# Block 1's branch projections and embedding gate: from three 256-column matmuls on a shared bank to 512+256 columns on a bank per feature tile

## The chip, the cores and the metric

The kernel runs on one core of a Trainium2 chip. The metric is the device time of one execution in microseconds (us), as the median of several runs; lower is better. The engines are TensorE (PE for its matmuls, PEld for its weight loads), VectorE (DVE), ScalarE (ACT), GpSimd (POOL) and SyncE (SP, which issues the DMAs here).

## The reference, cut to what matters

A sequence of 256 tokens with 1024 features goes through two different transformer blocks in float32 (the second has two layers). The change lies in the first block, behind its attention:

```python
y_a = o_a @ w_branch_diff[i]          # o_a: [256, 512], out of the differential attention
y_b = o_b @ w_branch_moba[i]          # o_b: [256, 512], out of the block attention
merged = sigmoid(g_a) * y_a + sigmoid(g_b) * y_b
x = x + merged @ w_out[i]
x = x + sigmoid(x @ w_ple_gate[i]) * (p[i] @ w_ple[i])
```

After it the second block begins with `h = rmsnorm(x, g_mix[0])` and its wide input projection.

## The kernel before

Activations lie transposed: features on the 128 partitions, in 8 tiles of 128 features, the 256 tokens along the row. Every float32 product is made of three: each operand is split into a rounded high part (`F32R`) and the low rest, and hi*hi + hi*lo + lo*hi is summed in PSUM. A `Pair` tile holds high and low part of an activation tile side by side, 512 columns in all.

The weights come as a stream of 189 chunks of 1 MB (`chunks`). For every chunk the loop at the end of `tile_blocks` issues, in this order: the split of the chunk two further on (`split`: per half chunk a copy to `wh` on ACT, L286, and a subtraction to `wl` on DVE, L287), the fetch of the chunk five further on (an SP DMA), then the chunk's matmuls and what empties their banks, then one step of each open attention head (`threads`). A planner that simulates the engines writes the final order of each engine's queue, so work of neighbouring chunks and heads is interleaved on PE, and that order is fixed when the kernel runs.

PSUM has five banks for the chunks (`acc`, `NACC`) and three for the heads (`aux`). A chunk's matmuls take one of these forms:

- `mm_2` (L308, used by `chunk_2`, `branch1` and `ple`): two feature tiles share one bank, 256 columns each. For each k tile and each of the two, `mm3` (L131 to L133) issues three matmuls of 256 columns, each with its own weight load: `wh` on the high part, `wh` again on the low part, `wl` on the high part. The bank then holds finished sums.
- `mm_t` (L292, used by `chunk_t`): a feature tile has a bank of its own. `wh` is loaded once and multiplies high and low part in one matmul of 512 columns (L300), `wl` multiplies the high part in one of 256 columns (L303). The sum for a token is then the sum of the bank's two halves, which `fold` makes: a copy of one half to SBUF on ACT (L320), and an addition of the other on DVE (L321). With `fresh` the two kinds alternate k tile by k tile, otherwise all 512-column ones come first.
- `mm_n` (L343): tokens on the partitions, for values and for keys and queries of block 1, always 512 columns.

Block 1 behind its attention: four chunks `branch1(c)`, each with two feature tiles of both branch projections (four k tiles each); the chunk `ple` (`p @ w_ple`); four chunks of `w_out`, whose emptying adds to the residual `X` and writes the new `X` as a `Pair` (tag A2) with `hilo` (L127, L128); four chunks of `w_ple_gate`; then block 2's first projections, which read the `Pair` X2 that `norm_tile` (L196, L197, and the squares at L205, L207) writes. Before the change, `branch1` multiplies the sigmoids `ga`, `gb` with the banks on DVE (L626, L627), adds them on POOL (L628) and splits the result (L127, L128), 512 columns at a time. `pleg_evac` takes the sigmoid of the bank on ACT (`act`, L114), multiplies it with the embedding term `pw` (L706) and adds it to `X` (L707), 512 columns at a time, and then calls `norm_tile` for both feature tiles. In block 2 the same merge is done in the other form, by `ret_evac` and `sb_evac` with `merge_tile` (L609, L610).

Of the kernel before, what the change touches and what calls it, by code (L numbers as in the profile page):

```python
# [12 lines left out]
AF = mybir.ActivationFunctionType  # L13
# [8 lines left out]
S = 256  # L22
D = 1024
KT = 8
# [52 lines left out]
def tile_blocks(ctx: ExitStack, tc: tile.TileContext, a: dict, out: bass.AP):  # L77
    nc = tc.nc
    V, A, G, T = nc.vector, nc.scalar, nc.gpsimd, nc.tensor
# [6 lines left out]
    def tl(shape, tag, dt=F32, bufs=1):  # L86
        uid[0] += 1
        return pool.tile([P] + list(shape), dt, tag=tag, bufs=bufs, name=f"{tag}_{uid[0]}")
# [12 lines left out]
    def acc():  # L101
        uid[0] += 1
        return psp.tile([P, 512], F32, tag="acc", bufs=NACC, name=f"acc_{uid[0]}")
# [3 lines left out]
    def act(o, i, func, **kw):  # L107

        need = "sigmoid" if func == AF.Sigmoid else "natural_log_exp"
        if table[0] != need:  # L110
            table[0] = need
            ld = A.preload_act_table_set(need + "_and_others")
            tc.stamp_issue_order_token(ld.ins, "act_table")
        ins = A.activation(o, i, func, **kw)  # L114
        tc.stamp_issue_order_token(ins.ins, "act_table")

    def f32(ap):
        return ap.bitcast(F32)
# [7 lines left out]
    def hilo(hi, lo, src):  # L126
        A.activation(hi, src, AF.Copy)  # L127
        V.tensor_sub(lo, src, f32(hi))  # L128

    def mm3(o, lh, ll, rh, rl, start, stop):  # L130
        T.matmul(o, lhsT=lh, rhs=rh, start=start, stop=False, skip_group_check=True)  # L131
        T.matmul(o, lhsT=lh, rhs=rl, start=False, stop=False, skip_group_check=True)  # L132
        T.matmul(o, lhsT=ll, rhs=rh, start=False, stop=stop, skip_group_check=True)  # L133
# [52 lines left out]
    def new_norm(g, sub=None):  # L186
        n = Norm()
        n.g, n.sub = g, sub
        n.x = Pair("X2")
        n.sq = tl([S], "sq")  # L190
        n.sq2 = tl([S], "M2") if sub is not None else None
        return n

    def norm_hilo(n, x, k):

        A.activation(n.x.h[:, k], x, AF.Copy, scale=n.g[:, k:k + 1])  # L196
        V.scalar_tensor_tensor(n.x.l[:, k], x, n.g[:, k:k + 1], f32(n.x.h[:, k]), ALU.mult, ALU.subtract)  # L197

    def norm_square(n, X, k):

        for sq, kw in ((n.sq, {}), (n.sq2, {"scale": n.sub[:, k:k + 1]} if n.sub is not None else {})):
            if sq is None:
                continue
            t = sq if k == 0 else tl([S], "f", bufs=NF)
            A.activation(t, X[:, k], AF.Square, **kw)  # L205
            if k:
                (V if k == KT - 1 else G).tensor_add(sq, sq, t)  # L207

    def norm_tile(n, X, k):
        norm_hilo(n, X[:, k], k)  # L210
        norm_square(n, X, k)
# [43 lines left out]
    chunks = []  # L255
# [10 lines left out]
    def wcols(w, c, k0=0, kt=KT, n=S):  # L266
        return w, k0 * P, kt, c * n
# [21 lines left out]
    def mm_t(ch, ks, xs, j0, evac, n=2):  # L289

        for j in range(n):
            ps, w = acc(), slice((j0 + j) * P, (j0 + j + 1) * P)
            kinds = [[(i, n) for i in range(len(ks)) for n in range(2)]] if ch.fresh else \
                [[(i, n) for i in range(len(ks))] for n in range(2)]
            for i, n_ in sum(kinds, []):
                k, x = ks[i], xs[i]
                if n_ == 0:
                    T.matmul(ps, lhsT=ch.wh[:, k, w], rhs=x.rearrange("p c t -> p (c t)"), start=i == 0, stop=False,  # L300
                             skip_group_check=True)
                else:
                    T.matmul(ps[:, 0:S], lhsT=ch.wl[:, k, w], rhs=x[:, 0], start=False, stop=i == len(ks) - 1,  # L303
                             skip_group_check=True)
            run_pre()
            evac(ps, j)

    def mm_2(ch, ks, xs, j0=0, n=2):  # L308

        ps = acc().rearrange("p (j t) -> p j t", j=2)  # L310
        for i, (k, x) in enumerate(zip(ks, xs)):
            for j in range(2):
                w = slice((j0 + j) * P, (j0 + j + 1) * P)
                mm3(ps[:, j], ch.wh[:, k, w], ch.wl[:, k, w], x[:, 0], x[:, 1], i == 0 and j == 0, i == len(ks) - 1)
        return ps

    def fold(ps, out=None):

        t = tl([S], "f", bufs=NF) if out is None else out
        A.activation(t, ps[:, S:2 * S], AF.Copy)  # L320
        V.tensor_add(t, t, ps[:, 0:S])  # L321
        return t
# [25 lines left out]
    def run_pre():  # L348
        while pre:
            with tc.high_priority():  # L350
                pre.pop(0)()

    def chunk_t(w, c, x, evac, k0=0, fresh=False):
        def go(ch):
            mm_t(ch, range(KT), [x().t[:, k] for k in range(KT)], 0, lambda ps, j: evac(ps, 2 * c + j))
        chunks.append(Chunk([wcols(w, c, k0)], go))
        chunks[-1].fresh = fresh

    def chunk_2(w, c, x, evac, k0=0):
        def go(ch):  # L360
            ps = mm_2(ch, range(KT), [x().t[:, k] for k in range(KT)])
            run_pre()
            evac(ps, c)
        chunks.append(Chunk([wcols(w, c, k0)], go))

    def chunk_n(w, c, x, evac, k0=0, parts=1):
        ps = []

        def go(ch):
            if not ps:  # L370
                ps.extend([acc() for _ in range(parts)] for _ in range(2))
                if ch is chunks[0]:
                    mm_k(ch, ps, x(), 0)
                    return
                for h in range(2):
                    mm_n(ch, ps[h], x(), 0, h)
                return
            for h in range(2):
                mm_n(ch, ps[h], x(), 4, h)
                run_pre()  # L380
                evac(ps[h] if parts > 1 else ps[h][0], h)
        for half in range(2):
            chunks.append(Chunk([wcols(w, c, k0 + 4 * half, 4, 512)], go, (4, 512)))


    class Values:
# [5 lines left out]
        def evac(self, ps, h):  # L392
            r = st.n.rc[h]
            A.activation(self.h[:, h], ps, AF.Copy, scale=r)
            V.scalar_tensor_tensor(self.l[:, h], ps, r, f32(self.h[:, h]), ALU.mult, ALU.subtract)
# [3 lines left out]
    X = tl([KT, S], "X")  # L399
    n0 = new_norm(g_norm)  # L400
    st.n = n0
    x_ = lambda: st.n.x
# [197 lines left out]
    def sig(store, c, i):  # L600
        s = store[(c, i)]
        if not s[1]:
            act(s[0], s[0], AF.Sigmoid)
            s[1] = True
        return s[0]

    def merge_tile(k, pb, ga, gb):
        t = fold(pb)
        V.tensor_mul(t, t, gb)  # L609
        V.tensor_add(t, t, ga)  # L610
        hilo(mg.x.h[:, k], mg.x.l[:, k], t)

    gates1 = {}
    mg = Norm()

    def start_merge():
        mg.x = Pair("M2")

    def branch1(c):
        def go(ch):  # L620
            if c == 0:
                start_merge()
            xs = [a1.t[:, k] for k in range(8)]
            ga, gb = sig(gates1, c, 0), sig(gates1, c, 1)
            pa, pb = mm_2(ch, range(4), xs[0:4]), mm_2(ch, range(4, 8), xs[4:8])
            V.tensor_mul(ga, ga, pa)  # L626
            V.tensor_mul(gb, gb, pb)  # L627
            G.tensor_add(ga, ga, gb)  # L628
            k = slice(2 * c, 2 * c + 2)
            hilo(mg.x.h[:, k], mg.x.l[:, k], ga)  # L630
            if c == 1:
                threads.append(ple_in())
        chunks.append(Chunk([wcols(("w_branch_diff", 0), c, 0, 4), wcols(("w_branch_moba", 0), c, 0, 4)], go))
# [12 lines left out]
    def ple_in():  # L646

        pn = scr[:, 0:512].rearrange("p (j t) -> p j t", j=2)
        load(pn, a["pt"])
        yield  # L650
        pt_.x = Pair("vh", 2)
        hilo(pt_.x.h, pt_.x.l, pn)
        yield
# [43 lines left out]
            if k % 2:  # L697
                yield

    def pleg_evac(ps, c):  # L700
        if c == 0:
            nxt.n = new_norm(gfm, g_fin)
        k = slice(2 * c, 2 * c + 2)
        t = tl([2, S], "sig", bufs=4)
        act(t, ps, AF.Sigmoid)
        V.tensor_mul(t, t, pw[:, k])  # L706
        V.tensor_add(X[:, k], X[:, k], t)  # L707
        for j in range(2):
            norm_tile(nxt.n, X, 2 * c + j)
        if c == 3:  # L710
            st.n = nxt.n
            pre.append(rotary_scales)
            threads.append(first_out())

    nxt = Norm()
    for c in range(4):
        chunk_2(("w_ple_gate", 0), c, x_, pleg_evac)


    def ret_head(h, j, qk, v, L):  # L720
# [374 lines left out]
```

## Time and profile before

| what | value |
|---|---|
| median of 3 runs | 1169.01 us (1168.88 to 1169.1) |
| profiled execution, its own time | 1168.73 us |
| its span, from the first instruction to the last | 1167.0 us |
| mean granted TensorE clock in it | 0.997 |
| PE busy | 1155.9 us, 99% of the span |
| DVE, ACT, POOL busy | 876.3, 707.4, 221.2 us (75%, 61%, 19%) |

The profiled execution is 0.28 us under the median, and 1.73 us of its time lie outside the span. In the rows, a matmul's busy time includes its way through the array, so successive matmuls overlap: the pace of PE is read from the distance of starts, not from durations. ACT and DVE rows overlap their neighbours slightly as well. A line such as L321 is that of a helper, which many callers share; the names of the tiles tell them apart.

### The profile page before, as it was taken

How to read it: one execution, taken by the hardware profiler on the slowest of the kernel's cores; microseconds unless marked ns; L12 is line 12 of the kernel's file. 1: busy time of each engine (PE TensorE's matmuls, PEld its weight loads, DVE VectorE, ACT ScalarE, POOL GpSimd, SP SyncE). 2: the span in 40 equal slices, each digit the busy share in tenths (PEclk: the TensorE clock that was granted, in tenths of full speed). 3: DMA queues.
4: the chain of work that ended last, by engine and by line, in shares of the span. 5: the costliest groups of instructions: out<-in, count | busy, mean ns of one | idle time of the engine just before them, and what ended most of it. 6: DMA issues, size and time to landing. Idle time of an engine off the chain costs nothing.

```text
span 1167.0 us, 17530 instructions
## 1 busy us (share of the span) xinstructions
PE 1155.9 (99%) x6642; PEld 1013.0 (87%) x6642; DVE 876.3 (75%) x1433; ACT 707.4 (61%) x1275; POOL 221.2 (19%) x242
## 2 busy tenths in 40 slices
PE   8999999999999999999999999999999999999997
PEld 6888889998888888888888888888888888888887
DVE  7766867778997766678877778987776677967664
ACT  6657656566567776556744646556777555846442
POOL 1014104015641122211000002652112112000001
PEclk9999999999999999999999999999999999999999
DMA  8544435545555444546555556454444555555541
GB/s 312 182 144 145 145 117 181 182 180 196 193 181 179 145 164 163 183 165 220 190 181 185 199 183 213 173 196 178 145 168 157 181 183 196 184 184 211 180 180 37
DMA packets 32164, 206.58 MB, mean 177 GB/s; under 512 B 3920, under 2 KB 6224, under 8 KB 8144
## 3 DMA queue, kind: packets, MB, share of 16 engines
q1 hardware_dynamic: 31936, 205.44, 49.3%
q8 instruction: 52, 0.85, 0.3%
q14 instruction: 32, 0.26, 0.1%
q10 hardware_dynamic: 144, 0.03, 0.0%
HBM read 202.31 MB, written 1.05 MB: 174 GB/s over the span
## 4 chain that ended last, share of the span: by engine, by line
PE 94%; DVE 4%; ACT 1%; issue 1%; DMA 0%; POOLq 0%; POOL 0%; DVEq 0%
PE acc L300 41%; PE acc L303 21%; PE acc L343 20%; DVE wl L287 2%; PE aux L131 2%; PE aux L133 2%; PE aux L132 2%; PE acc L133 1%; PE acc L132 1%; PE acc L131 1%; DVE X L666 1%; PE aux L466 1%; PE aux L773 1%; DVE X L197 1%; PE acc L331 1%
## 5 line engine op out<-in xcount | busy, mean ns | idle before, releaser
L287 DVE TENSOR_TENSOR wl<-raw,wh 128x1024 fp32r<-128x1024 f32 (+1 forms) x380 | 462.8, 1249 | 135.1 <-ACT wh L286 130.4
L286 ACT ACTIVATE wh<-raw 128x1024 fp32r<-128x1024 f32 (+1 forms) x380 | 380.4, 1047 | 198.7 <-PE acc L300 109.0
L300 PE MATMUL acc<-X,wh 128*128 128x512 f32 x1472 | 383.1, 394 | 0.6 <-DVE X L666 0.4
L300 PEld LDWEIGHTS acc<-X,wh 128*128 128x128 f32 x1472 | 263.5, 189 | 47.9 <-issue 1.2
L303 PE MATMUL acc<-X,wl 128*128 128x256 f32 x1472 | 221.5, 283 | 0.0
L303 PEld LDWEIGHTS acc<-X,wl 128*128 128x128 f32 x1472 | 206.8, 190 | 13.6
L320 ACT ACTIVATE f<-acc 128x256 f32<-128x256 f32 x216 | 79.4, 374 | 61.8 <-PE acc L303 61.6
L343 PE MATMUL acc<-wh,X 128*128 128x512 f32 x432 | 111.8, 392 | 0.5 <-DVE f L321 0.5
L321 DVE TENSOR_TENSOR f<-f,acc 128x256 f32<-128x256 f32 x216 | 87.7, 414 | 24.0 <-ACT f L320 22.1
L343 PEld LDWEIGHTS acc<-wh,X 128*128 128x128 f32 x432 | 80.0, 188 | 16.6 <-DVE f L321 0.7
L207 POOL TENSOR_TENSOR sq<-sq,f 128x256 f32<-128x256 f32 x30 | 31.5, 1051 | 274.7 <-ACT f L205 274.3
L666 DVE TENSOR_TENSOR X<-X,acc 128x256 f32<-128x256 f32 x112 | 45.8, 416 | 34.2 <-PE acc L303 33.6
L597 POOL TENSOR_TENSOR sig<-f,nr 128x256 f32<-128x256 f32 x48 | 40.9, 859 | 147.1 <-DVE f L321 122.0
L300 PE MATMUL acc<-A,wh 128*128 128x512 f32 x256 | 64.5, 393 | 0.0
L300 PE MATMUL acc<-B,wh 128*128 128x512 f32 x256 | 64.4, 392 | 0.0
L343 PE MATMUL acc<-wl,X 128*128 128x512 f32 x216 | 60.0, 393 | 0.0
L300 PEld LDWEIGHTS acc<-B,wh 128*128 128x128 f32 x256 | 46.1, 189 | 8.2
L300 PE MATMUL acc<-M,wh 128*128 128x512 f32 x192 | 53.0, 394 | 0.0
L300 PEld LDWEIGHTS acc<-A,wh 128*128 128x128 f32 x256 | 46.0, 189 | 8.1
L343 PEld LDWEIGHTS acc<-wl,X 128*128 128x128 f32 x216 | 40.0, 188 | 7.8
L300 PEld LDWEIGHTS acc<-M,wh 128*128 128x128 f32 x192 | 35.0, 188 | 6.9
L303 PEld LDWEIGHTS acc<-A,wl 128*128 128x128 f32 x256 | 35.1, 190 | 2.5
(224 smaller groups left out, 1687.0 us busy)
## 6 DMA issues: line engine op xcount, KB each, us to landing
raw<-in_wstream_dram SPq DMA_DIRECT2D x187, 1024.0 KB, 4.8
raw<-in_wstream_dram SPq DMA_DIRECT2D x4, 512.0 KB, 7.8
sig<-f SPq DMA_DIRECT2D x32, 64.0 KB, 4.6
B<-in_tables_dram SPq DMA_DIRECT2D x2, 768.0 KB, 6.0
X<-in_xt_dram SPq DMA_DIRECT2D x2, 512.0 KB, 6.3
out_dram<-M SPq DMA_DIRECT2D x4, 256.0 KB, 2.2
M<-in_g_final_dram SPq DMA_DIRECT2D x1, 512.0 KB, 4.5
cst<-in_tables_dram SPq DMA_DIRECT2D x1, 352.0 KB, 10.2
```

The source lines that it names most:

```text
L131: T.matmul(o, lhsT=lh, rhs=rh, start=start, stop=False, skip_group_check=True)
L132: T.matmul(o, lhsT=lh, rhs=rl, start=False, stop=False, skip_group_check=True)
L133: T.matmul(o, lhsT=ll, rhs=rh, start=False, stop=stop, skip_group_check=True)
L286: A.activation(ch.wh[:, k], ch.raw[:, k], AF.Copy)
L287: V.tensor_sub(ch.wl[:, k], ch.raw[:, k], f32(ch.wh[:, k]))
L300: T.matmul(ps, lhsT=ch.wh[:, k, w], rhs=x.rearrange("p c t -> p (c t)"), start=i == 0, stop=False, skip_group_check=True)
L303: T.matmul(ps[:, 0:S], lhsT=ch.wl[:, k, w], rhs=x[:, 0], start=False, stop=i == len(ks) - 1, skip_group_check=True)
L320: A.activation(t, ps[:, S:2 * S], AF.Copy)
L321: V.tensor_add(t, t, ps[:, 0:S])
L343: T.matmul(p[:, 0:w], lhsT=xs[:, k, t], rhs=ws[:, i, o], start=n == 0 and k == 0, stop=n == 2 and k == KT - 1, skip_group_check=True)
L597: G.tensor_mul(store[(c, i)][0][:, k % 2], fold(ps), st.n.rb)
L666: V.tensor_add(X[:, k], X[:, k], ps[:, o:o + S])
```

## The change

The four `branch1` chunks and the four `w_ple_gate` chunks go from `mm_2` to `mm_t`; `chunk_2` goes. In `branch1`, each of the two projections is done for one feature tile after the other, on a bank each: `first` folds the bank of the first projection and multiplies it with `ga` on POOL, `second` hands the bank of the second to `merge_tile`, which folds, multiplies, adds and splits it at 256 columns. `pleg_evac` is called for each feature tile: `fold`, then the sigmoid in place, product, sum and `norm_tile`, all at 256 columns. The first gate chunk is `fresh`. `ple` keeps `mm_2`.

```diff
--- before.py
+++ after.py
@@ -356,13 +356,6 @@
         chunks.append(Chunk([wcols(w, c, k0)], go))
         chunks[-1].fresh = fresh
 
-    def chunk_2(w, c, x, evac, k0=0):
-        def go(ch):
-            ps = mm_2(ch, range(KT), [x().t[:, k] for k in range(KT)])
-            run_pre()
-            evac(ps, c)
-        chunks.append(Chunk([wcols(w, c, k0)], go))
-
     def chunk_n(w, c, x, evac, k0=0, parts=1):
         ps = []
 
@@ -622,12 +615,15 @@
                 start_merge()
             xs = [a1.t[:, k] for k in range(8)]
             ga, gb = sig(gates1, c, 0), sig(gates1, c, 1)
-            pa, pb = mm_2(ch, range(4), xs[0:4]), mm_2(ch, range(4, 8), xs[4:8])
-            V.tensor_mul(ga, ga, pa)
-            V.tensor_mul(gb, gb, pb)
-            G.tensor_add(ga, ga, gb)
-            k = slice(2 * c, 2 * c + 2)
-            hilo(mg.x.h[:, k], mg.x.l[:, k], ga)
+
+            def first(ps, j):
+                G.tensor_mul(ga[:, j], ga[:, j], fold(ps))
+
+            def second(ps, j):
+                merge_tile(2 * c + j, ps, ga[:, j], gb[:, j])
+
+            mm_t(ch, range(4), xs[0:4], 0, first)
+            mm_t(ch, range(4, 8), xs[4:8], 0, second)
             if c == 1:
                 threads.append(ple_in())
         chunks.append(Chunk([wcols(("w_branch_diff", 0), c, 0, 4), wcols(("w_branch_moba", 0), c, 0, 4)], go))
@@ -697,24 +693,22 @@
             if k % 2:
                 yield
 
-    def pleg_evac(ps, c):
-        if c == 0:
+    def pleg_evac(ps, k):
+        if k == 0:
             nxt.n = new_norm(gfm, g_fin)
-        k = slice(2 * c, 2 * c + 2)
-        t = tl([2, S], "sig", bufs=4)
-        act(t, ps, AF.Sigmoid)
+        t = fold(ps)
+        act(t, t, AF.Sigmoid)
         V.tensor_mul(t, t, pw[:, k])
         V.tensor_add(X[:, k], X[:, k], t)
-        for j in range(2):
-            norm_tile(nxt.n, X, 2 * c + j)
-        if c == 3:
+        norm_tile(nxt.n, X, k)
+        if k == KT - 1:
             st.n = nxt.n
             pre.append(rotary_scales)
             threads.append(first_out())
 
     nxt = Norm()
     for c in range(4):
-        chunk_2(("w_ple_gate", 0), c, x_, pleg_evac)
+        chunk_t(("w_ple_gate", 0), c, x_, pleg_evac, fresh=c == 0)
 
 
     def ret_head(h, j, qk, v, L):
```

## Rows read from the trace of the kernel before

**Rows 1.** Page, part 1: busy time, share of the span, instructions

```profile
span 1167.0 us, 17530 instructions
...
PE 1155.9 (99%) x6642; PEld 1013.0 (87%) x6642; DVE 876.3 (75%) x1433; ACT 707.4 (61%) x1275; POOL 221.2 (19%) x242
```

**Rows 2.** Chain that ended last, 225 to 285 us: start, length, step

```profile
by line: PE acc L300 27.3%; PE acc L343 18.2%; PE acc L303 14.4%; PE acc L131 12.8%; PE acc L132 12.8%; PE acc L133 12.8%; PE aux L223 1.1%; PE aux L220 1.0%
...
226.50 1.84 PE acc L300 x8
228.34 0.95 PE acc L303 x8
...
262.61 2.72 PE acc L343 x12
```

**Rows 3.** Timeline of PE, block 1's embedding gate: start, length, group of matmuls

```profile
234.72 0.28 PE L131 MATMUL acc<-A,wh 128*128 128x256 f32 x1
...
252.00 0.28 PE L131 MATMUL acc<-A,wh 128*128 128x256 f32 x1
...
252.36 0.28 PE L131 MATMUL acc<-A,wh 128*128 128x256 f32 x1
...
257.76 0.40 PE L300 MATMUL acc<-X,wh 128*128 128x512 f32 x1
...
258.11 0.40 PE L300 MATMUL acc<-X,wh 128*128 128x512 f32 x1
```

**Rows 4.** Stretches: us, then busy PE, PEld, DVE, ACT, POOL (instructions), PEclk, DMA share, GB/s

```profile
196.00:208.00 12.00, 12.00 (x102) 12.00 (x102) 8.57 (x11) 7.15 (x10) 3.14 (x5) 1.00 0.57 203
208.00:214.00 6.00, 6.00 (x48) 5.78 (x47) 4.28 (x4) 4.47 (x7) 0.95 (x1) 1.00 0.55 194
...
226.34:231.92 5.58, 5.58 (x34) 4.91 (x33) 4.44 (x9) 2.73 (x4) 0.00 (x0) 1.00 0.51 188
...
238.60:268.60 30.00, 30.00 (x215) 28.30 (x215) 23.84 (x27) 20.42 (x38) 10.70 (x12) 1.00 0.56 202
...
252.00:257.76 5.76, 5.76 (x51) 5.76 (x50) 5.46 (x6) 4.70 (x9) 2.67 (x4) 1.00 0.49 188
```

**Rows 5.** Groups by line and shape: busy, mean ns of one

```profile
L320 ACT ACTIVATE f<-acc 128x256 f32<-128x256 f32 x216 | 79.4, 374 | 61.8 <-PE acc L303 61.6
...
L321 DVE TENSOR_TENSOR f<-f,acc 128x256 f32<-128x256 f32 x216 | 87.7, 414 | 24.0 <-ACT f L320 22.1 <-POOL sig L870 0.9
...
L609 DVE TENSOR_TENSOR f<-f,sig 128x256 f32<-128x256 f32 x16 | 7.8, 490 | 0.3
...
L610 DVE TENSOR_TENSOR f<-f,sig 128x256 f32<-128x256 f32 x16 | 7.5, 469 | 1.6
...
L627 DVE TENSOR_TENSOR sig<-sig,acc 128x512 f32<-128x512 f32 x4 | 2.7, 682 | 0.3 <-PE acc L133 0.3
...
L706 DVE TENSOR_TENSOR sig<-sig,B 128x512 f32<-128x512 f32 x4 | 3.3, 825 | 0.0
...
L707 DVE TENSOR_TENSOR X<-X,sig 128x512 f32<-128x512 f32 x4 | 3.8, 958 | 0.1
...
L114 ACT ACTIVATE sig<-acc 128x512 f32<-128x512 f32 x4 | 2.3, 579 | 0.0
...
L114 ACT ACTIVATE f<-G 128x256 f32<-128x256 f32 x24 | 9.7, 415 | 19.1 <-POOL G L546 19.0
```

**Rows 6.** Timeline of DVE, embedding gate and its end

```profile
237.86 0.76 DVE L128 TENSOR_TENSOR A<-X,A 128x256 fp32r<-128x256 f32 x2
243.38 2.36 DVE L287 TENSOR_TENSOR wl<-raw,wh 128x1024 fp32r<-128x1024 f32 x2 [4.77 <-ACT wh L286]
...
263.17 3.60 DVE L197 SCALAR_TENSOR_TENSOR X<-X,gfm,X 128x256 fp32r<-128x256 f32 x4
```

**Rows 7.** Timeline of PE, block 2's first switch to the up-projection

```profile
533.25 2.48 PE L300 MATMUL acc<-X,wh 128*128 128x512 f32 x10
535.92 1.63 PE L300 MATMUL acc<-X,wh 128*128 128x512 f32 x6 [0.19 <-DVE X L666]
```


## The prediction

> **What bounds the kernel now.** I read the first part of the page first: PE is busy for 1155.9 of 1167.0 us, against 876.3 on DVE and 707.4 on ACT [rows 1]. That alone doesn't say that PE sets the end, because a matmul's record reaches beyond the start of the next, so I read the chain of waits next. Between 225 and 285 us, which holds the whole embedding gate and the step into block 2, it consists of matmuls only [rows 2]. The windows say the same: PE is busy for the full length of each stretch, at a granted clock of 1.00, the upper of its two levels (2.4 GHz) [rows 4]. So in the changed stretch time is what PE needs to issue its matmuls, and work on other engines costs something only if it makes PE wait.
>
> **The pace of the two forms.** In the timeline of PE, three matmuls of 256 columns start 0.12 us apart, so one k tile of one feature tile takes 0.36 us [rows 3]. A gate chunk has 8 k tiles by 2 feature tiles, 16 such triples: 5.76 us, which is the stretch from 252.00 to 257.76 [rows 3, 4]. Weight loads are busy there for 5.76 of 5.76 us. In the other form the chain shows eight 512-column matmuls in 1.84 us and eight of 256 columns in 0.95 [rows 2]: 2.79 us for a feature tile, 5.58 for two, which is the stretch from 226.34 to 231.92; weight loads are busy for 4.91 of it [rows 4]. The columns streamed are the same, 768 per k tile and feature tile. What goes is one of three matmul starts with its weight load, and it is worth 5.76 - 5.58 = 0.18 us a chunk.
>
> The Trainium skill (TensorE: Matmul & The Clock Gate, Back-to-back issue gap) gives a warm matmul its columns over 2.4 GHz plus 2.5 ns, so that a matmul saved would be worth 2.5 ns. By that the 128 triples would give an estimated 0.32 us. The trace does not agree: 0.18 us over 16 triples is 11 ns each, and the measured rows are used below.
>
> **The sum on PE.** A branch chunk has 4 k tiles by 2 feature tiles by 2 projections, again 16 triples, so each of the eight chunks has 48 matmuls before and 32 after. Seven of them take the order of all 512-column matmuls first: 7 x 0.18 = 1.26 us. No row shows it with four k tiles in a row instead of eight; I take the same pace. The first gate chunk is fresh. In that order a pair takes 258.11 - 257.76 = 0.35 us [rows 3], 16 of them 5.60, which saves 0.16. Together -1.42 us. Bounds: nothing, if the columns alone decide; and -1.86 if 512 columns go at the pace of the value chunk, 2.72 / 12 = 0.227 us [rows 2], which makes a feature tile 8 x 0.227 + 0.95 = 2.76 us, a chunk 5.53 and eight chunks 8 x 0.23.
>
> **The new wait.** The first gate chunk starts on PE at 234.72, right behind w_out [rows 3]. Its last k tile is the end of w_out's evacuation: DVE writes the low halves of the last two tiles of A2 from 237.86 on, until 238.62 [rows 6]. The old form does both feature tiles k tile by k tile and needs the last at 234.72 + 14 x 0.36 = 239.76, late enough. The new one does the first feature tile alone and needs it at 234.72 + 7 x 0.35 = 237.17, 1.45 us too early, and the second feature tile and everything behind it stand in PE's queue. The planner can put the second tile's first six k tiles in between (12 pairs reach 234.72 + 4.20 = 238.92), and then nothing is lost. Its habit is seen at block 2's switch to the up-projection, the same situation: ten 512-column matmuls are drawn forward there, which at 0.23 us end at 535.55, and the next starts at 535.92 after a wait for DVE's X [rows 7]. I take that 0.37 us, with bounds 0 and 1.45.
>
> **The evacuation, on DVE and ACT.** It is hidden behind PE unless it grows past it.
> - Branch chunk: four folds (0.374 ACT, 0.414 DVE each) come in, and two products of 0.49 and two sums of 0.47 in place of two products of 0.682 from the bank [rows 5]. DVE gains 1.66 + 0.98 + 0.94 - 1.36 = 2.2 us, ACT 1.5. The split into high and low is the same work in halves; POOL exchanges a sum of 512 columns for two products of 256. In 196 to 208, which holds the two branch chunks with no gate projection between them, DVE has 8.57 of 12 us [rows 4]. It would need 13.0 and be 1.0 late. The next in need of it is w_out, and `ple` stands between with 48 matmuls of 0.12 us, 5.76 us, where DVE has 1.7 us free in 208 to 214 [rows 3, 4]. Cost: nothing. Without `ple` in between it would be that 1.0 us and the chain of the last tile.
> - Gate chunk: two folds, two sigmoids of 0.415 in place of one of 0.579, and two products and sums of about 0.48 in place of 0.825 and 0.958 [rows 5]. ACT and DVE each gain 1.0 us a chunk, 4 us over four. In 238.6 to 268.6 DVE has 23.84 of 30 us and ACT 20.42 [rows 4], and 4.77 us of what DVE has free lie at the start, where it has no finished bank yet [rows 6]. A bank per feature tile is finished half a chunk earlier, so the added work can go there. The end of it is DVE's last low half, 263.17 + 3.60 = 266.77 [rows 6]. That is 9.0 us after the last gate matmul, and PE covered these 9 us with block 2's first chunks on the five banks without a gap [rows 2, 4]. Cost: nothing, as long as the 9 us don't grow.
> - Transfers: weights, their order and their sizes stay. No DMA is added.
>
> **The sum.** 1168.73 (profiled execution) - 1.42 + 0.37 = 1167.68. The median of the runs is 0.28 above that execution, so the forecast is 1168.0 us, 0.09% less. This kernel's measurement can tell about 0.2% from no change, 2.34 us: no difference. From the bounds alone (-1.86 to 0, and 0 to 1.45) this case gives 1167.2 to 1170.5.
>
> **Rivals.**
> 1. *DVE becomes the bound at the end of the embedding gate (slower).* If the 4.77 us at the start can't be used, because the bank is folded only behind the splits in DVE's queue, DVE has 23.84 + 4.77 + 3.9 = 32.5 us of work and wait in 30, and the last tile has a fold more in its chain (0.374 + 0.414). Then block 2's input is 2.5 + 0.8 = 3.3 us later, the five banks are full, and PE waits: 1168.0 + 3.3 = 1171.3. Beyond that point, 3.4 us, it is slower by over 0.2%. For it: sums that read two SBUF tiles are long here, 0.958 at L707 against 0.682 for a product of the same size that reads PSUM [rows 5]. Were the 16 new products and sums longer by that ratio, 0.48 x 0.4 x 16 = 3.1 us would come on top: 1174.4. Against it: the spare 6.2 us of DVE in the stretch. I take 1172.0.
>  The Trainium skill (GPSIMD Engine Reference) says that POOL shares its SBUF interfaces with VectorE and contends with DVE instructions of two SBUF inputs. By that, folds, which read PSUM, are spared and the new sums aren't; the two rows agree in direction, and no row here separates POOL's part.
> 2. *The planner writes another order.* Changed lengths move its choices in the rest of block 1 and perhaps in block 2. For it: the order is mixed across chunks, as the ten matmuls drawn forward show [rows 7]. Against: PE is full anyway, with 11.1 us idle in all [rows 1]. I price it at three waits of 0.37 more or fewer: 1166.9 or 1169.1, and three times that at the worst.
> 3. *More pace than assumed (faster).* The value chunk's pace and no new wait: 1169.01 - 1.86 = 1167.15. To pass 0.2% another 0.5 us has to come from the planner's order: 1166.5.
> 4. *The form changes nothing*, because the columns decide: 1169.0, or 1169.4 with the new wait.
>
> **How the numbers follow.** Forecast 0.57, rival 1 0.14, rival 2 0.17, rival 3 0.07, rival 4 0.05. Faster by over 0.2% are most of rival 3 and a quarter of rival 2, 0.10. Slower by over 0.2% are most of rival 1 (0.11) and a fifth of rival 2 (0.03): 0.14. No difference: 0.76. For 8 in 10 the range goes from rival 3's far end with something of rival 2 below it, 1166.2, to just short of rival 1's 1171.3: 1171.0.
>
> **What would show it.** Right: PE has 128 matmuls fewer; L131 to L133 on A tiles are gone; 16 pairs take about 5.6 us; the first gate chunk's k tiles show a gap or drawn-forward matmuls around 237; PE stays full through the step into block 2. Wrong: a gap on PE that ends with DVE's L197, L321 or L707 between 255 and 275 (rival 1); gaps or another order after 285 us (rival 2); a tile of eight pairs that isn't 2.8 us long (rivals 3 and 4).

## The result and the profile after

The changed kernel takes 1182.63 us (1182.39 to 1184.77), the kernel before 1169.05 on the same chip: a ratio of 1.0119, 95% interval 1.0107 to 1.0132. It is 13.6 us slower, where 1168.0 was forecast and 1171.0 was the upper end of the range.

Part 1 of the page of after, the answer to [rows 1]:

```profile
span 1180.6 us, 17373 instructions
...
PE 1159.0 (98%) x6514; PEld 1007.5 (85%) x6514; DVE 882.1 (75%) x1477; ACT 714.9 (61%) x1307; POOL 217.3 (18%) x246
```

There are 128 matmuls fewer, as there should be. Span less busy PE was 11.1 us and is 21.6. On every other engine the busy time moved by under 8 us, so the page says only that PE now waits; it doesn't say where.

**Where.** I cut the span by the start of the first matmul that reads a given tile, taken from the timelines of PE:

| stretch, from one first matmul to the next | before, us | after, us |
|---|---|---|
| branch projections to `w_out` of block 1 | 149.03 to 212.32: 63.3 | 149.14 to 215.94: 66.8 |
| `w_out` to the embedding gate | 22.4 | 22.4 |
| embedding gate to `w_out_2` of block 2's first layer | 234.72 to 507.29: 272.6 | 238.32 to 520.92: 282.6 |
| from there to the end of the span | 659.7 | 659.7 |

The branch stage lost 3.5 us, the gate with the step into block 2 10.0 us; nothing moved elsewhere.

**The gate.** The timeline of PE in after, at the rows that begin a feature tile or stand behind a wait (in brackets the idle time before the row and what ended it; X is the tile X2, and L701 and L702, further down, are the product and the sum that were L706 and L707 before):

```profile
252.35 2.00 PE L300 MATMUL acc<-A,wh 128*128 128x512 f32 x8
254.19 1.11 PE L303 MATMUL acc<-A,wl 128*128 128x256 f32 x8
255.14 2.00 PE L300 MATMUL acc<-A,wh 128*128 128x512 f32 x8
...
259.77 2.08 PE L300 MATMUL acc<-A,wh 128*128 128x512 f32 x8 [1.67 <-DVE f L321]
261.69 1.11 PE L303 MATMUL acc<-A,wl 128*128 128x256 f32 x8
...
263.10 0.47 PE L300 MATMUL acc<-X,wh 128*128 128x512 f32 x1 [0.30 <-DVE f L321]
...
267.76 0.50 PE L300 MATMUL acc<-X,wh 128*128 128x512 f32 x1 [3.36 <-DVE X L197]
...
268.75 0.77 PE L300 MATMUL acc<-X,wh 128*128 128x512 f32 x1 [0.38 <-DVE f L321]
...
274.43 0.50 PE L300 MATMUL acc<-X,wh 128*128 128x512 f32 x1 [0.80 <-DVE X L197]
...
277.77 0.50 PE L300 MATMUL acc<-X,wh 128*128 128x512 f32 x1 [0.73 <-DVE X L197]
```

A feature tile takes 255.14 - 252.35 = 2.79 us, exactly the predicted pace. Then PE waits six times, 7.24 us in all: three times for a fold, because all five banks are full, and three times for the next k tile of X2. Before, PE had no such gap here [rows 2, 4].

The chain of waits of after, 262 to 272 us, by line, and one of its turns:

```profile
by line: DVE wl L287 23.6%; ACT f L205 18.1%; ACT X L196 10.2%; ACT wh L286 9.6%; DVE X L702 8.7%; DVE f L321 8.6%; ACT f L114 8.5%; ACT f L320 8.2%; DVE f L701 7.8%; issue 2.3%
...
267.89 0.28 ACT f L320
...
268.19 0.43 DVE f L321
...
268.64 0.42 ACT f L114
...
269.09 0.44 DVE f L701
...
269.55 0.44 DVE X L702
...
270.01 0.51 ACT X L196
270.52 0.70 ACT f L205 x2
271.22 0.28 ACT f L320
```

Where [rows 2] has matmuls only, there is no matmul left. One feature tile goes through all its steps, fold, sigmoid, product, sum, high half, squares, and only then does the fold of the next begin. A turn takes 3.33 us (267.89 to 271.22), PE needs 2.79 for a tile, and the weight splits (L286, L287) come on top where they fall into it. ACT's row shows that the next fold was not waiting for its bank (timeline of ACT in after):

```profile
261.74 0.49 ACT L205 ACTIVATE f<-X,gc 128x256 f32<-128x256 f32 x1
262.14 0.36 ACT L320 ACTIVATE f<-acc 128x256 f32<-128x256 f32 x1
...
267.39 0.49 ACT L205 ACTIVATE f<-X,gc 128x256 f32<-128x256 f32 x1
267.79 0.36 ACT L320 ACTIVATE f<-acc 128x256 f32<-128x256 f32 x1
```

No wait stands before L320; from the third fold on it follows a square directly, each time. The last gate matmuls start at 261.69, so every bank folded from 267.79 on was full long before. It is the order of ACT's queue that holds the fold back. The windows, first of before, from DVE's first split of the gate [rows 6] to the end of its last low half, then of after, from the first fold to the end of its last low half (columns as in [rows 4]):

```profile
243.38:266.77 23.39, 23.39 (x167) 21.96 (x166) 22.63 (x24) 19.11 (x36) 9.39 (x11) 1.00 0.53 192
```

```profile
247.84:281.41 33.57, 26.32 (x134) 21.50 (x133) 23.05 (x41) 23.66 (x49) 9.22 (x12) 0.95 0.38 130
...
267.70:272.30 4.60, 4.16 (x14) 3.39 (x15) 2.18 (x6) 2.67 (x8) 2.68 (x4) 0.63 0.44 183
```

DVE has the same 23 us of work as before, spread over 33.6 us, and ACT 23.7: neither is full, the two wait for each other in turn. The line of before shows something else too: from its first split on, DVE was busy for 22.63 of 23.39 us, so its free time in the gate lay almost wholly ahead of that split. The last gate matmuls are issued by 261.69 + 8 x 0.12 = 262.65, the last low half of X2 ends at 281.41: 18.8 us, where the prediction counted on 9.0.

The second row of after shows a follow-up. Behind the wait of 3.36 us the granted clock is 0.63 in the mean of 4.6 us, so for a part of them it was at the lower of its two levels (1.2 and 2.4 GHz). Five pairs take from 268.75 to 271.96, 3.21 us, against 5 x 0.35 = 1.75 [rows 3]. So 7.2 us of waits, 1.0 that the marked idle time leaves out (it counts from a matmul's modelled end, 0.16 us behind the pace, six times), 1.5 of clock, less 0.7 of better pace: 9.0 of the 10.0 us.

**The branch projections.** The timeline of PE in after has four gaps here, before none:

```profile
159.65 0.39 PE L131 MATMUL aux<-ph,vh 128*128 128x256 f32 x1 [0.74 <-ACT B L114]
...
176.67 0.50 PE L300 MATMUL acc<-A,wh 128*128 128x512 f32 x1 [1.49 <-DVE A L128]
...
178.64 2.11 PE L300 MATMUL acc<-X,wh 128*128 128x512 f32 x8 [0.29 <-DVE f L321]
...
182.12 1.20 PE L300 MATMUL acc<-A,wh 128*128 128x512 f32 x4 [0.42 <-DVE f L321]
```

And the folds (L320) on ACT from 154 to 182 us, first in the timeline of before, then of after:

```profile
164.73 0.37 ACT L320 ACTIVATE f<-acc 128x256 f32<-128x256 f32 x1
...
168.47 0.36 ACT L320 ACTIVATE f<-acc 128x256 f32<-128x256 f32 x1
...
173.54 0.38 ACT L320 ACTIVATE f<-acc 128x256 f32<-128x256 f32 x1 [1.31 <-PE acc L303]
...
178.01 0.36 ACT L320 ACTIVATE f<-acc 128x256 f32<-128x256 f32 x1
```

```profile
154.92 0.38 ACT L320 ACTIVATE f<-acc 128x256 f32<-128x256 f32 x1 [0.66 <-PE acc L303]
...
177.68 0.38 ACT L320 ACTIVATE f<-acc 128x256 f32<-128x256 f32 x1 [1.67 <-PE acc L303]
179.86 1.19 ACT L320 ACTIVATE f<-acc 128x256 f32<-128x256 f32 x4
```

The first chunk's second projection needs the last attention head, so its banks stay open until then. Before, gate projections of the same stretch were folded meanwhile. In after no fold runs for over 22 us, finished banks stay full, and then the folds come together: first the two of the second branch projection (177.68 and the first at 179.86), and only behind them three of gate projections.

### The profile page after: what moved, and what is told of

It reads as the page before. It is cut to its first block, busy times and chain, and to the rows that moved or that the text cites. A ratio compares the mean times of both kernels' runs of the same rounds, so it can differ in the third digit from the quotient of the medians.

```text
span 1180.6 us, 17373 instructions
## 1 busy us (share of the span) xinstructions
PE 1159.0 (98%) x6514; PEld 1007.5 (85%) x6514; DVE 882.1 (75%) x1477; ACT 714.9 (61%) x1307; POOL 217.3 (18%) x246
## 4 chain that ended last, share of the span: by engine, by line
PE 91%; DVE 5%; ACT 2%; issue 1%; DMA 0%; POOLq 0%; POOL 0%; DVEq 0%; ACTq 0%
PE acc L300 42%; PE acc L303 21%; PE acc L343 19%; DVE wl L287 2%; PE aux L131 2%; PE aux L132 2%; PE aux L133 2%; DVE X L662 1%; PE aux L459 1%; PE acc L331 1%; PE aux L767 1%; ACT wh L286 1%; DVE X L197 0%; DMA X<-in_xt_dram 0%; ACT X L196 0%
## 5 line engine op out<-in xcount | busy, mean ns | idle before, releaser
L287 DVE TENSOR_TENSOR wl<-raw,wh 128x1024 fp32r<-128x1024 f32 (+1 forms) x380 | 461.6, 1245 | 126.1 <-ACT wh L286 121.4
L286 ACT ACTIVATE wh<-raw 128x1024 fp32r<-128x1024 f32 (+1 forms) x380 | 380.2, 1047 | 187.0 <-PE acc L300 105.7
L303 PEld LDWEIGHTS acc<-X,wl 128*128 128x128 f32 x1472 | 207.7, 190 | 13.6
L320 ACT ACTIVATE f<-acc 128x256 f32<-128x256 f32 x240 | 87.7, 374 | 76.9 <-PE acc L303 73.9
L321 DVE TENSOR_TENSOR f<-f,acc 128x256 f32<-128x256 f32 x240 | 97.1, 413 | 33.3 <-ACT f L320 31.3
L300 PE MATMUL acc<-A,wh 128*128 128x512 f32 x384 | 100.8, 394 | 3.6 <-DVE f L321 2.1
L300 PEld LDWEIGHTS acc<-A,wh 128*128 128x128 f32 x384 | 68.2, 189 | 15.8 <-DVE A L128 1.9
L303 PEld LDWEIGHTS acc<-A,wl 128*128 128x128 f32 x384 | 54.4, 190 | 4.5
L303 PE MATMUL acc<-A,wl 128*128 128x256 f32 x384 | 57.1, 282 | 0.0
```

The lines of the kernel that those rows point to most:

```text
L286: A.activation(ch.wh[:, k], ch.raw[:, k], AF.Copy)
L287: V.tensor_sub(ch.wl[:, k], ch.raw[:, k], f32(ch.wh[:, k]))
```

## The experiments

Theory A: the new folds take their tile from the tag `f` (`tl([S], "f", bufs=NF)`), from which `norm_square` and the gate projections' folds take theirs too, and the queues keep a tag's tiles in the order in which the program asks for them. So a fold that comes late holds back work that doesn't need its result. The rivals: B, DVE's added work (the prediction's first rival); C, named in the expectation of experiment 3, the fresh order, which opens all five banks before the first is finished, so that the evacuation starts late; D, the number of the tag's buffers. Kernel n is the kernel of experiment n. Each was timed beside the kernel before (1169.24 to 1169.37 us there), which its ratio refers to. Ahead of the changed stages the profiled executions differ by up to 2.0 us (the first branch matmul starts between 149.0 and 151.1 us), so I compare the lengths of the two stages, read from each run as in the table above.

**1 and 2. One half of the change each**, against after: first the gate as it was, then the branch chunks as they were.

```diff
-        chunk_t(("w_ple_gate", 0), c, x_, pleg_evac, fresh=c == 0)
+        chunk_2(("w_ple_gate", 0), c, x_, pleg_evac)      # kernel 1, with the old pleg_evac
...
-            mm_t(ch, range(4), xs[0:4], 0, first)
-            mm_t(ch, range(4, 8), xs[4:8], 0, second)
+            pa, pb = mm_2(ch, range(4), xs[0:4]), mm_2(ch, range(4, 8), xs[4:8])      # kernel 2, with the old evacuation
```

> The branch chunks in the new form, the embedding gate as before. In the trace of after, a fixed point of PE (the start of the embedding gate) is 3.6 us later than before, and a fixed point in block 2 13.6 us later. Theory A (order of the f tiles: all folds and all squares share one tag of six buffers, which the planner hands out in program order, so that a fold cannot be queued ahead of work that the program has before it) and theory B (the evacuation is too much work for DVE and ACT in the gate) both expect the two parts to add: A 1172.6 us (1172.0 to 1173.5). B, in which the branch costs nothing by itself, 1168.4.

> The embedding gate in the new form, the branch chunks as before. A and B: 1179 us (1178 to 1180), the 10.0 us that lie between the start of the gate and block 2. If the branch's delay brings the gate out of step, less: 1170 to 1175.

Branch alone: 1172.58 us, ratio 1.0029 (1.0019 to 1.0039), the branch stage 66.8 us. Gate alone: 1180.08, 1.0089 (1.0072 to 1.0106), the gate stretch 282.3 us. Each half is slower by itself, and with the change as it is the two about add up: 3.3 and 10.8 us, against 13.6 together.

**3. The gate's fold on a tag of its own**, the one that its sigmoid had before.

```diff
-        t = fold(ps)
+        t = fold(ps, tl([S], "sig", bufs=4))
```

> As after, but the gate's folds take their tile from the tag sig, which is free there and which the old form used, in place of f. No work is added or taken away. A: the folds and sigmoids of later feature tiles go ahead of the squares of earlier ones, PE's gaps between 257 and 278 us go, and the time falls by 9 to 10.5 us to 1173 (1172 to 1175). B: the same work takes the same time, 1181 to 1183. Theory C (the fresh order opens five banks before the first is finished, so that evacuation starts 6 us late and never catches up): about half, 1177, because the late start stays.

1177.83 us, ratio 1.0072 (1.0057 to 1.0087); the gate stretch takes 277.0 us: 5.6 of the 10.0 us are gone by the name of a tag. ACT's queue, as it is written into the program, shows how, first in after, then here (names shortened; the number behind a name rises in the order in which the program asked for the tiles):

```
L320 ACTIVATE f_2538<-acc_2521 128x256
L114 ACTIVATE f_2538<-f_2538 128x256
L196 ACTIVATE X2_2469<-X_79,gfm_76 128x256
L205 ACTIVATE f_2546<-X_79 128x256
L205 ACTIVATE f_2549<-X_79,gc_61 128x256
L320 ACTIVATE f_2569<-acc_2552 128x256
```

```
L320 ACTIVATE sig_2608<-acc_2591 128x256
L114 ACTIVATE sig_2569<-sig_2569 128x256
L196 ACTIVATE X2_2469<-X_79,gfm_76 128x256
L205 ACTIVATE f_2507<-X_79 128x256
L205 ACTIVATE f_2510<-X_79,gc_61 128x256
L320 ACTIVATE sig_2639<-acc_2622 128x256
```

In after the numbers of `f` only rise: fold 2569 stands behind squares 2546 and 2549. Here fold 2608 stands ahead of square 2507. Theory A's mechanism is shown, and it isn't the whole: 4.4 us of the gate remain, and the time misses A's 1172 to 1175 us. It is close to the 1177 that theory C named, in which the late start stays.

**4. Own tags for the branch folds too**, on kernel 3 (tags `t`, `cr` and `sr`, which nothing else uses then; `merge_tile` hands the tile on to `fold`).

```diff
-                G.tensor_mul(ga[:, j], ga[:, j], fold(ps))
+                G.tensor_mul(ga[:, j], ga[:, j], fold(ps, tl([S], "t", bufs=2)))
...
-                merge_tile(2 * c + j, ps, ga[:, j], gb[:, j])
+                merge_tile(2 * c + j, ps, ga[:, j], gb[:, j], tl([S], ("cr", "sr")[j]))
```

> As e3, and the branch's folds too take tiles outside f (t, cr and sr, which block 2 alone uses). A: the queue of ACT can put the folds of the gate projections ahead of those of the second branch product, the 3.6 us of the branch go as well, and what is left is the gain in PE's pace: 1168.0 us (1167.2 to 1169.5). B: 1178 or more. If the branch's delay has another cause (two open banks more while the attention heads finish), 1171.5 to 1173.

1175.83 us, ratio 1.0052 (1.0037 to 1.0067), between what A (1168.0) and B (1178 or more) expected. The branch stage falls from 66.8 to 64.1, the gate stays at 277.0. Of the gaps of the branch stage only the first is left. Two windows of this run, the first from DVE's first fold of the gate to the last low half, and PE's wait for X2 in its timeline:

```profile
247.20:273.64 26.44, 23.36 (x123) 19.71 (x122) 25.73 (x40) 22.71 (x48) 10.85 (x12) 0.94 0.52 186
...
265.00:270.00 5.00, 4.92 (x17) 4.11 (x18) 5.00 (x11) 3.25 (x7) 3.31 (x4) 0.68 0.56 210
```

```profile
265.08 0.80 PE L300 MATMUL acc<-X,wh 128*128 128x512 f32 x1 [2.92 <-DVE X L197]
```

Now DVE is full, 25.73 of 26.44 us, with 3.1 us more to do than before. That is rival B, which the order of the queues had hidden. The stretch also begins later: the gate's first matmul starts at 237.28 here, so DVE's first fold is 9.9 us behind it, where before its first split was 8.7 us behind (243.38 - 234.72). 1.3 us of later start and 3.0 us of longer stretch put the last low half 4.3 us later, which is about what remains of the gate's loss.

**5. Seven buffers for the tag `f`**, with the change as it is.

```diff
-NF = 6
+NF = 7
```

> As after, with seven f buffers in place of six. Theory A (the tag is handed out in program order, so that a fold waits for the squares of the feature tile before it, however many buffers there are): no change from after, 1182.5 us (1181 to 1184), and on ACT each fold from the third on still stands behind the two squares of the tile before. The rival, that six buffers are too few for the folds that are now in flight: 1177 or less, as with the tag of their own.

1182.46 us, ratio 1.0114 (1.0098 to 1.0129), the gate stretch 282.65 us: no change. The order is the cause, not the count: theory D falls. The Trainium skill (Perfetto Trace Analysis, Optimization Strategy) takes a gap that repeats on the engine that should be full as a sign that there may be too few buffers; for these gaps and the buffers of `f` this run says otherwise.

**6 and 7. What DVE's share is worth**, on kernel 4: the gate's product on POOL, or left out.

```diff
-        V.tensor_mul(t, t, pw[:, k])
+        G.tensor_mul(t, t, pw[:, k])      # kernel 6; kernel 7 has no such line
```

> As the kernel with tags of their own for both folds (1175.8 us), with the gate's product with the embedding term on POOL in place of DVE. In that kernel DVE is busy for 25.73 of 26.44 us from the first fold to the last low half. Theory B for what is left (DVE is the bound there): DVE loses 8 x 0.35 = 2.8 us, the gap of 2.9 us on PE before block 2 shrinks to 0.5 or less, and with it the stretch at the lower clock goes: 1171.5 (1170.5 to 1173.5). If the chain of waits from engine to engine is the bound, the product takes 0.74 in place of 0.42 there and nothing is gained: 1175.5 to 1178.

> As the kernel with tags of their own, with the gate's product with the embedding term left out (its output is not the reference's): the eight products on DVE go, nothing else. B: 1171.0 us (1170 to 1173). Beside the kernel with the product on POOL it shows what POOL's use of the time costs. If DVE's work doesn't decide, 1175 to 1176.

On POOL: 1175.97 us, ratio 1.0056 (1.0041 to 1.0071), nothing gained; the product takes 0.79 to 1.72 us there, DVE's remaining sums 0.94 in the median, and the wait for X2 is 3.86 us. B's 1171.5 is missed, and the number is the one that a chain of waits from engine to engine would give. The window of kernel 6, from DVE's first fold to the last low half, speaks for B all the same: without the eight products DVE is still nearly full, because what is left takes longer.

```profile
246.65:273.24 26.59, 22.59 (x118) 18.85 (x117) 25.25 (x33) 22.60 (x49) 21.16 (x20) 0.94 0.49 181
```

Left out: 1172.06, 1.0029 (1.0018 to 1.004), the gate stretch 274.1 us, as B expected. This takes 3.5 us of work from DVE and also a step from the chain of each feature tile, so by itself it doesn't tell the two apart. The waits of PE in kernel 7 and in the last experiment, 12:

```profile
264.68 0.50 PE L300 MATMUL acc<-X,wh 128*128 128x512 f32 x1 [1.84 <-DVE X L197]
```

```profile
263.95 0.50 PE L300 MATMUL acc<-X,wh 128*128 128x512 f32 x1 [2.27 <-DVE X L197]
```

**8, 10 and 11. The branch half by itself.** Kernel 8: first branch chunk and gate old, chunks 1 to 3 new. Kernel 10: all four branch chunks new on tags of their own, gate old. Kernel 11: kernel 8 with own tags.

```diff
+            if c == 0:      # kernels 8 and 11
+                pa, pb = mm_2(ch, range(4), xs[0:4]), mm_2(ch, range(4, 8), xs[4:8])
...
+            else:
                 mm_t(ch, range(4), xs[0:4], 0, first)
                 mm_t(ch, range(4, 8), xs[4:8], 0, second)
```

> The first branch chunk and the whole gate as before, branch chunks 1 to 3 in the new form with their folds in f. The theory that the branch's loss lies where the first chunk stands open until the last attention head has finished, with the folds of the next gate projections queued behind its folds: the loss goes, 1168.7 us (1168.0 to 1169.7), with 0.5 us of gain from the pace of three chunks. If each chunk in the new form costs its evacuation: 1171.5 to 1172.5.

> The branch chunks in the new form with their folds in t, cr and sr, the gate as before. If the order of the f tiles caused the branch's 3.3 us: 1168.5 us (1167.8 to 1169.7). By the difference of the two runs with and without these tags beside the new gate (2.0 us) only part of it: 1170.6 (1169.8 to 1171.5).

> Branch chunks 1 to 3 in the new form with their folds in t, cr and sr, the first branch chunk and the gate as before. It leaves out both places that were seen to lose time. If the pace of three chunks is gained and nothing else lost: 1168.7 us against 1169.24, a gain of 0.5 (0 to 1). If the wait of 0.8 us for a fold ahead of branch chunk 2 stays, as in the run with these folds in f: 1170.0 to 1170.8.

They take 1170.55, 1170.45 and 1170.45 us, ratios 1.0011 (1.0002 to 1.002), 1.0009 (0.9999 to 1.0018) and 1.001 (1.0001 to 1.0019). Their branch stages are 63.9, 64.1 and 63.9 us against 66.8 with the change as it is, so the folds of the first chunk, in the shared tag, made most of the 3.5 us. A rest of 0.65 to 0.85 us stays in each, in a stage that has less matmul time than before, and none comes down to the 1168.5 to 1168.7 us that I expected if nothing but the order of the first chunk's folds cost time. Part is seen: kernel 10 keeps one gap of 0.73 us behind ACT's L114 in an attention head, kernels 8 and 11 one of 0.83 and 0.85 behind L321. No version beats the kernel before.

**9. The gate alone on its own tag**: kernel 2 with the edit of kernel 3.

```diff
-        t = fold(ps)
+        t = fold(ps, tl([S], "sig", bufs=4))
```

> The gate in the new form with its folds in sig, the branch chunks as before. If the parts add, the kernel with both in the new form and the gate's folds in sig (1177.8) less the branch's own 3.3 us: 1174.5 us (1173.3 to 1175.5), about 5 over before, all of it DVE's added work at the end of the gate and the clock behind the gap. If the tag was all, 1168.5.

1176.51 us, ratio 1.0061 (1.0048 to 1.0075), 2 us above what I expected. The gate stretch takes 278.9 us, where it takes 277.0 with the new branch form ahead of it; PE waits 4.67 us for X2, with a granted clock of 0.50 from 265 to 270. So with tags of their own the halves don't simply add up. The order of the gate's work on DVE is another one here than in kernel 4; why it is the worse one I did not find.

**12. POOL's share.** On kernel 4, six of POOL's sums of squares left out.

```diff
-            if k:
+            if k and (sq is n.sq or k == KT - 1):
```

> As the kernel with tags of their own for both folds (1175.8 us), with six of POOL's twelve sums of squares in the gate left out (the sum that the first norm's own scale is taken from; the output is then not the reference's). DVE's instructions are the same. If POOL at work slows DVE's instructions with two SBUF inputs (0.96 us against 0.42 for the sum with X in that kernel) and DVE is the bound: 1173.5 us (1172.5 to 1175). If POOL plays no part: 1175.5 to 1176.5.

1173.88 us, ratio 1.0042 (1.0028 to 1.0055); the gate stretch falls from 277.0 to 276.0 us. DVE's work is the same as in kernel 4 by the program, but its sums and low halves are shorter (L197, ns of one, min/median/max, in kernel 4 and in this one, from the view by line):

```profile
L197 DVE SCALAR_TENSOR_TENSOR X<-X,gfm,X x8: 478/956/1039, 258.1 to 272.8; 128x256 fp32r<-128x256 f32 x8
```

```profile
L197 DVE SCALAR_TENSOR_TENSOR X<-X,gfm,X x8: 472/486/969, 258.1 to 271.1; 128x256 fp32r<-128x256 f32 x8
```

## Why the prediction was wrong, point by point

- *What bounds the kernel, and the pace of PE: right.* A gate tile takes 2.79 us, 128 matmuls are gone. In the branch chunks, four k tiles of both kinds start 1.40 to 1.41 us apart (kernel 10: 199.35, 200.76, 202.16), so a chunk takes 5.62 us and saves 0.14 instead of 0.18. The gain of about 1.3 us is there, under waits ten times its size.
- *The new wait of 0.37 us at the first gate chunk: not seen.* PE has no gap between 238.32 and 257.9 us. Matmuls of other tiles are drawn forward (five and twelve in a row at 241.15 and 242.76). The price shows elsewhere: the first bank is finished later (below).
- *The gate's evacuation, "cost: nothing, as long as the 9 us don't grow": the step that failed.* The added 4 us of work were about right (DVE has 3.1 more in kernel 4), and so was the condition. The 9.0 us grew to 18.8, and that cost 10.0 us. I had compared work with time on DVE and ACT, as if their instructions could be put in any order. Two things in it were wrong.
  First, the tile that `fold` takes. In the kernel before, bank and sigmoid's tile belonged to the gate alone. The new `fold` draws on the tag that `norm_square` uses twice for every feature tile, and so the fold that frees the next bank stands behind a chain of 3.3 us: 5.6 us of the 10.0 (kernel 3 against after).
  Second, "a bank per feature tile is finished half a chunk earlier, so the added work can go there". The first bank is finished later. Rows of PE and ACT before, then of ACT and DVE in after:

```profile
242.04 0.40 PE L133 MATMUL acc<-A,wl 128*128 128x256 f32 x2
...
242.28 2.01 ACT L286 ACTIVATE wh<-raw 128x1024 fp32r<-128x1024 f32 x2 [5.03 <-PE acc L132]
244.20 0.58 ACT L114 ACTIVATE sig<-acc 128x512 f32<-128x512 f32 x1
```

```profile
247.84 0.38 ACT L320 ACTIVATE f<-acc 128x256 f32<-128x256 f32 x1 [6.97 <-PE acc L303]
...
248.26 0.42 DVE L321 TENSOR_TENSOR f<-f,acc 128x256 f32<-128x256 f32 x1 [5.71 <-ACT f L320]
```

  Before, in the order of the program's matmuls, the last one for the first bank is the one at 242.04, so two feature tiles are finished at 242.32, 7.6 us after the gate's first matmul; their sigmoid stands behind a weight split on ACT until 244.20. In after matmuls of all five banks are drawn forward, and the fold of the first bank, with one feature tile, waits for PE until 247.84, 9.5 us after the first matmul. DVE sits idle for 5.71 us ahead of it, and behind the start DVE had hardly any free time even before (22.63 of 23.39 us). So the added work lands at the end: 4.4 us remain in kernel 4. No run has the first gate chunk in the other order of matmuls, so what the late start costs by itself (theory C) is read from rows and not tested.
- *Rival 1 (DVE becomes the bound), chance 0.14, 1171.3 to 1174.4 us: right as the second mechanism.* It put the last tile 3.3 us later, or 6.4 with longer sums; in kernel 4 it is 4.3. Its condition, that the free time at the start can't be used, came true, but because the bank is finished late and not because of the splits. It left out what a wait brings along: in kernel 4 the granted clock is 0.68 from 265 to 270 us. Kernel 7, which takes eight products from DVE, wins 2.9 us of the 4.4.
- *The longer sums of two SBUF tiles* (3.1 us in rival 1): the effect exists, but rival 1 mis-sized it. Its 0.958 is the mean of two sums of 0.69 and two of 1.22. Of the 16 new products and sums in kernel 4 only three took over 0.43 us (0.62, 0.96, 0.96), 1.3 us more in all. The low halves L197 are long in kernel 4, but they were as long before; only in after, where the same POOL work is spread over a longer time, they are short, 0.48 in the median. By line, L707 and L197 before, then the product and the sum in kernel 4 (ns of one, min/median/max):

```profile
L707 DVE TENSOR_TENSOR X<-X,sig x4: 691/957/1225, 246.4 to 262.6; 128x512 f32<-128x512 f32 x4
...
L197 DVE SCALAR_TENSOR_TENSOR X<-X,gfm,X x8: 479/957/1036, 250.3 to 265.8; 128x256 fp32r<-128x256 f32 x8
```

```profile
L701 DVE TENSOR_TENSOR sig<-sig,B x8: 410/417/615, 250.9 to 270.1; 128x256 f32<-128x256 f32 x8
...
L702 DVE TENSOR_TENSOR X<-X,sig x8: 410/418/959, 252.7 to 270.6; 128x256 f32<-128x256 f32 x8
```

  The Trainium skill (GPSIMD Engine Reference, 1. Specifications) says that POOL contends with DVE instructions of two SBUF inputs. The traces agree: kernel 12, with less on POOL, brings the median of L197 back from 0.96 to 0.49.
- *The branch's evacuation, "cost: nothing": wrong by 3.5 us.* I looked for its cost behind the last chunk, where `ple` covers it, as it does (`w_out` to the gate is 22.4 us in both). The cost arose at the first chunk, whose folds wait for the last attention head and hold back the gate projections' folds in the same tag: 2.7 to 2.9 us by kernels 4, 8, 10 and 11. The rest is open.
- *Rivals 2 to 4:* from `w_out_2` of block 2's first layer on, both kernels take 659.7 us, so another order in the rest (rival 2) didn't move the time; a feature tile of 2.79 us leaves no room for rivals 3 and 4.

## What to carry to other kernels

Before a step is moved to a helper, ask which tag the helper draws its tiles from and who else draws from it: where tiles of a tag are handed out in program order, a shared tag ties work together that the data leaves free, and one buffer more did not help here. Free time on an engine covers added work only if a row shows that the work's input is there when the time is free; busy shares of a stretch don't say that. And where PE is full, a wait can be dearer than its length: behind most of the long ones here the granted clock fell.

## What the runs showed of the hardware

- In the gate of kernel 4, DVE's instructions of two SBUF inputs at 128x256 took 0.41 to 0.43 us (product, sum) or 0.48 (low half) with no POOL sum at work beside them. Beside one, some took as long, some 0.62, and most 0.94 to 1.04. The fold, which reads one input from PSUM, took 0.41 to 0.42 throughout.
- Behind PE's longest gap in the gate the granted clock fell: to 0.63 in after (3.36 us), and from 265 to 270 us to 0.68 in kernel 4 (2.92 us), 0.50 in kernel 9 (4.67 us) and 0.69 in kernel 12 (2.27 us); in kernel 6 (3.86 us) it was 0.78. A 512+256 pair took 0.64 us in after instead of 0.35. Behind kernel 7's gap of 1.84 us it stayed at 1.00. A long gap isn't the only occasion: in kernel 7 the clock was 0.50 from 158.1 to 161.5 us, among the small matmuls of the attention heads, and the branch stage took 64.7 us there instead of kernel 4's 64.1.
- Moving the gate's product to POOL saved nothing: it took 1.54 us there in the median, against 0.42 on DVE, and DVE's sums beside it took 0.94 in the median instead of 0.42.
